# Opening of a two-block transformer layer: the first RMS norm moved behind the transposes and behind the products

## The chip, the cores and the metric

The kernel runs on 1 core of one Trainium2 chip. The core has TensorE (PE, with its weight loads PEld), VectorE (DVE), ScalarE (ACT), GpSimd (POOL) and SyncE (SP, which here only issues transfers), which run side by side and wait for each other by semaphores. The metric is the device time of one execution in microseconds (us); the kernel before takes 884.37 us as the median of 3 runs (884.16 to 885.26).

## The reference, cut to what matters

Two blocks follow each other. Only the head of the first is touched:

```python
def rmsnorm(x, g):
    y = x * lax.rsqrt(jnp.mean(x * x, axis=-1, keepdims=True) + EPS) * g
    return y

h = rmsnorm(x, g_mix_pre[l])            # x: 256 tokens x 1024, f32
proj = h @ w_in[l]                      # 1024 x 3080
# columns of proj: fq 512 | fk 512 | fv 512 | f_logit 8 | cq 512 | ck 512 | cv 512
y_fox = forgetting_attention(fq, fk, fv, f_logit + b_fgt)
y_chk = chunked_relpos_attention(cq, ck, cv, rel_bias)
```

After that come an output projection, attention over a memory, a feed-forward part, and a second block that is as long again. A token's factor 1/rms is one number per row of `h`, so it can be taken out of the product: `h @ w = (1/rms) * ((x * g) @ w)`.

## The kernel before

Everything is float32, and a product is made of three passes of a reduced format: each operand is split into a high part and the rest (hi, lo), and `mm3` issues hi x hi, hi x lo and lo x hi. ACT makes the hi part (a cast), DVE the lo part (a subtraction that reads the hi part). The weights come as units of 512 or 520 KB: SP loads a unit into one of four `raw` buffers, ACT makes `whi`, DVE makes `wlo`, and the buffer is free for the fourth unit after it. The 256 tokens are two halves, A and B, of 128 each; `ht` (tile `xb`) holds `h` transposed, eight tiles kt = 0 to 7 of 128 features, hi and lo.

The Python code is only the text from which a program is recorded: a small planner (`Kern`) keeps an estimate of each engine's clock and decides where the steps of side chains (norms, attention heads) are put between the products. The recorded order is fixed, each engine runs its own list strictly in order, and waits are semaphores. All instructions except products (L212, `mm`) and transposes (L225, `tr`) carry the line of one helper, L96, so groups are told apart by tile names.

The opening of `block1` in the kernel before, in order:

- SP loads the gain row `grow`, half B of `x`, and four units of `w_in`; ACT's queue loads half A of `x`.
- PE copies the gain to all partitions by a product with ones (`gb`). ACT squares and sums each half, POOL makes 1/rms (`rs`), DVE makes `xg` = x * rs * gain.
- PE transposes `xg`, 16 tiles of 128x128 into four PSUM banks (`tb`). ACT and DVE split each bank with one instruction each (128x512).
- Unit 0 is split by ACT and POOL, the other units by ACT and DVE.
- `gemm_n_skew` computes fv and f_logit (tile `gs`, two banks of 260 columns): four units for half A, then the same four for half B, 96 products in all.

Then the columns come in the order fq, fk (`gemm_t`, tile `gt`, results `qk`, each unit 24 products of 256 columns), cv (`gemm_n_inter`, tile `gn`), cq, ck (`gt`), and the two attentions run as side chains between the products. The forget gates need a running sum, `cps`, whose split form `ncum` enters the scores `s` of the first attention. ACT carries the results of fq, fk, cq and ck out of PSUM (`qk_evac`) and scales the queries by 0.125.

Of the kernel before, what the change touches and what calls it, by code (L numbers as in the profile page):

```python
# [21 lines left out]
EPS = 1e-6  # L22
N4, N2, NRAW = 33, 13, 4
# [15 lines left out]
def hs(half):  # L39
    return slice(half * P, half * P + P)  # L40
# [668 lines left out]
def block1(k, x, mem, w_in, b_fgt, rel, g_fox_out, g_chk_out, w_out, g_mix_pre, g_mix_post,  # L709
# [14 lines left out]
    gb = [k.bank(name="gb") for _ in range(2)]
    for j in range(2):
        k.mm(gb[j], k.ones[0:1, :], grow[:, j * 512:j * 512 + 512])
    xg, rs = [], []
    for half in range(2):
        xg.append(k.t4([P, D], name="xg"))
        ss, r = k.small(1, "ss"), k.small(1, "rs")  # L730
        nc.scalar.activation(xg[half], x0[half], AF.Square, scale=D ** -0.5, accum_out=ss)
        nc.gpsimd.tensor_tensor(r, ss, k.eps, op=OP.add)
        nc.gpsimd.tensor_tensor(r, r, k.mhalf[:, :1], op=OP.pow)
        rs.append(r)
    u = k.units
    k.split_hi(u[0])
    for kt in range(2):
        nc.gpsimd.tensor_tensor(u[0].lo[:, kt], u[0].raw[:, kt], u[0].hi[:, kt].bitcast(F32), op=OP.subtract)
    k.split_done()

    def norm_t(half, j):

        c = slice(j * 512, j * 512 + 512)
        nc.vector.scalar_tensor_tensor(xg[half][:, c], x0[half][:, c], rs[half], gb[j], op0=OP.mult, op1=OP.mult)
        ps = k.bank((P, 4, P), "tb")
        for i in range(4):
            k.tr(ps[:, i], xg[half][:, j * 512 + i * P:j * 512 + i * P + P])
        return ps

    def split_t(half, j, ps):  # L750
        split(k, ht.hi[j][:, :, hs(half)], ht.lo[j][:, :, hs(half)], ps)
        k.put()
    ps = [norm_t(half, j) for half in range(2) for j in range(2)]
    k.put(2)
    split_t(0, 0, ps[0])
    split_t(0, 1, ps[1])
    k.split_hi(u[1])
    k.split_lo(u[1])
    split_t(1, 0, ps[2])
    split_t(1, 1, ps[3])  # L760
    k.pump()
    setup_late(k)
# [10 lines left out]
    nc.gpsimd.memset(sp, 0.0)  # L773
# [3 lines left out]
    def fv_evac(half, j, ps):  # L777
        nc.scalar.copy(fv[:, half, 0:260], ps[0][:, :260])
        nc.scalar.copy(fv[:, half, 260:512], ps[1][:, :252])

        nc.vector.scalar_tensor_tensor(nx[:, half], ps[1][:, 252:260], -1.0, bf, op0=OP.mult, op1=OP.subtract)
        nc.vector.scalar_tensor_tensor(ax[:, half], nx[:, half], -1.0, nx[:, half], op0=OP.mult, op1=OP.min)


    gemm_n_skew(k, ht, 1, fv_evac, width=260, nb=2)
# [134 lines left out]
    gemm_n_inter(k, ht, lambda half, ps: nc.scalar.copy(cv[:, half], ps[0]))  # L920
# [986 lines left out]
```

## Time and profile before

| | us |
|---|---|
| median of 3 runs | 884.37 |
| the profiled execution | 884.47 |
| its span, first to last instruction | 882.7 |
| PE busy | 871.3 |
| DVE busy | 608.7 |
| ACT busy | 457.1 |
| POOL busy | 92.2 |

The profiled execution's own time is 1.8 us above its span; that rest lies around the instructions. Times in the rows count from the start of the span. The share of a busy PE says little by itself, because products are pipelined and their ends are modelled; what ends last is read from the chain of waits and from the idle time before single instructions.

### The profile page before, as it was taken

What the parts mean: (1) busy time and instruction counts of PE and PEld (TensorE: products, weight loads), DVE (VectorE), ACT (ScalarE), POOL (GpSimd) and SP (SyncE); (2) the same over time, 40 slices, a digit from 0 to 9 for tenths busy, and PEclk for the clock granted to TensorE, in tenths of its full rate; (3) what the DMA queues carried; (4) which work ended last, traced back from release to release, by engine and by line L of the source; (5) the groups of instructions that cost most, each with busy time, mean ns of one, the idle gap of its engine ahead of it and who ended that gap; (6) DMA issues with size and microseconds to landing.
All of it is one profiled execution on the core that took longest, in us unless ns stands there. A gap on an engine that the chain in (4) does not pass through costs nothing.

```text
span 882.7 us, 13878 instructions
## 1 busy us (share of the span) xinstructions
PE 871.3 (99%) x5320; PEld 754.4 (85%) x5320; DVE 608.7 (69%) x1076; ACT 457.1 (52%) x803; POOL 92.2 (10%) x150
## 2 busy tenths in 40 slices
PE   8999999999999999999999999999999999999998
PEld 6979998799788888888798899988987888888887
DVE  5675664765687667664769999979579786666661
ACT  6674654554476444442656665554564654444440
POOL 3101010200020000000100039800010000000000
PEclk9999999999999999999999999999999999999999
DMA  8992436473277766654551677395125586666521
GB/s 267 290 256 73 144 120 239 119 245 116 95 240 217 210 200 191 191 191 146 171 160 49 192 174 197 87 248 166 51 72 185 178 250 198 191 191 191 191 96 48
DMA packets 162612, 150.82 MB, mean 171 GB/s; under 512 B 20081, under 2 KB 127217, under 8 KB 162546
## 3 DMA queue, kind: packets, MB, share of 16 engines
q1 hardware_dynamic: 161970, 148.88, 56.7%
q10 hardware_dynamic: 576, 1.05, 0.4%
q8 instruction: 42, 0.69, 0.3%
q14 instruction: 24, 0.20, 0.1%
HBM read 148.08 MB, written 1.84 MB: 170 GB/s over the span
## 4 chain that ended last, share of the span: by engine, by line
PE 90%; DVE 4%; ACT 4%; issue 1%; DMA 0%; POOL 0%; DVEq 0%; ACTq 0%; POOLq 0%
PE gt L212 33%; PE acc L212 20%; PE gs L212 12%; PE gn L212 11%; PE tb L225 3%; PE mo L212 3%; DVE wlo L96 2%; PE o L212 1%; ACT whi L96 1%; ACT p L96 1%; ACT junk L96 1%; PE ops L212 1%; PE ms L212 1%; PE s L212 1%; DVE Z L96 1%
## 5 line engine op out<-in xcount | busy, mean ns | idle before, releaser
L96 DVE TENSOR_TENSOR wlo<-raw,whi 128x1024 fp32r<-128x1024 f32 (+1 forms) x263 | 316.4, 1225 | 107.6 <-ACT whi L96 98.6
L96 ACT CAST whi<-raw 128x1024 fp32r<-128x1024 f32 (+1 forms) x264 | 270.0, 1049 | 66.0 <-DMA raw<-in_w_in_dram 30.8
L212 PE MATMUL gt<-xb,whi 128*128 128x256 f32 (+1 forms) x1152 | 276.3, 322 | 0.0
L212 PE MATMUL gt<-xb,wlo 128*128 128x256 f32 x768 | 214.9, 280 | 0.0
L212 PEld LDWEIGHTS gt<-xb,whi 128*128 128x128 f32 x1152 | 190.0, 188 | 17.8 <-issue 1.0
L212 PEld LDWEIGHTS gt<-xb,wlo 128*128 128x128 f32 x768 | 144.6, 188 | 0.3
L212 PE MATMUL acc<-wlo,uh 128*128 128x512 f32 (+1 forms) x288 | 106.2, 369 | 0.0
L212 PE MATMUL acc<-whi,ul 128*128 128x512 f32 (+1 forms) x288 | 106.2, 369 | 0.0
L212 PE MATMUL acc<-whi,uh 128*128 128x512 f32 (+1 forms) x288 | 106.0, 368 | 0.0
L212 PE MATMUL gn<-whi,xb 128*128 128x512 f32 x256 | 90.8, 409 | 0.0
L212 PE MATMUL gs<-whi,xb 128*128 128x512 f32 (+1 forms) x288 | 85.8, 374 | 0.5 <-ACT xb L96 0.5
L212 PEld LDWEIGHTS acc<-whi,uh 128*128 128x128 f32 x288 | 54.2, 188 | 10.1
L212 PEld LDWEIGHTS acc<-whi,ul 128*128 128x128 f32 x288 | 54.1, 188 | 9.7
L212 PEld LDWEIGHTS acc<-wlo,uh 128*128 128x128 f32 x288 | 54.1, 188 | 9.6
L212 PEld LDWEIGHTS gs<-whi,xb 128*128 128x128 f32 x288 | 52.0, 188 | 10.9 <-ACT xb L96 1.0
L96 ACT COPY r<-gt 128x256 f32<-128x256 f32 x48 | 17.8, 371 | 83.5 <-PE gt L212 83.5
L212 PEld LDWEIGHTS gn<-whi,xb 128*128 128x128 f32 x256 | 48.2, 188 | 10.5 <-issue 0.7
L96 DVE TENSOR_TENSOR r<-gt,r 128x256 f32<-128x256 f32 x48 | 20.3, 423 | 49.3 <-ACT r L96 48.7
L212 PE MATMUL gs<-wlo,xb 128*128 128x512 f32 (+1 forms) x144 | 53.4, 371 | 0.8 <-DVE wlo L96 0.7
L96 POOL TENSOR_SCALAR ms<-ss 128x1 f32<-128x1 f32 x20 | 9.2, 458 | 420.4 <-ACT junk L96 420.3
L212 PE MATMUL gn<-wlo,xb 128*128 128x512 f32 x128 | 50.4, 394 | 0.0
L212 PEld LDWEIGHTS gs<-wlo,xb 128*128 128x128 f32 x144 | 27.1, 188 | 5.7 <-DVE wlo L96 1.4
(378 smaller groups left out, 1218.1 us busy)
## 6 DMA issues: line engine op xcount, KB each, us to landing
raw<-in_w_in_dram SPq DMA_DIRECT2D x84, 512.0 KB, 4.6
raw<-in_w_ff_dram SPq DMA_DIRECT2D x64, 512.0 KB, 4.6
raw<-in_w_mlp_up_dram SPq DMA_DIRECT2D x32, 512.0 KB, 5.4
raw<-in_w_mlp_down_dram SPq DMA_DIRECT2D x32, 512.0 KB, 3.4
raw<-in_w_out_dram SPq DMA_DIRECT2D x16, 512.0 KB, 3.9
raw<-in_w_mk_dram SPq DMA_DIRECT2D x8, 512.0 KB, 5.3
raw<-in_w_mv_dram SPq DMA_DIRECT2D x8, 512.0 KB, 4.0
raw<-in_w_mq_dram SPq DMA_DIRECT2D x8, 512.0 KB, 4.7
```

Source lines behind the costliest of these rows:

```text
L96: f(*args, **kw)
L212: self.nc.tensor.matmul(out, lhsT, rhs, start=start, stop=stop)
L225: self.nc.tensor.transpose(out, in_, self.ident[:n, :n])
```

## The change

The norm of the opening is taken apart.

- `x` is transposed as it comes (8 transposes of half A, later 8 of half B). The gain is loaded as 8 rows of 128 (`g8`), transposed once, and kept as `gT`, one number per partition and kt. It is applied when a transposed tile is split: ACT writes hi = tile * g, DVE writes lo = tile * g - hi. The split is now one 128x128 tile at a time.
- The weights of unit 0 are split in two halves, by ACT and DVE, between the tiles of half A; the lo part of unit 1 is made by POOL.
- Unit 0's load goes ahead of half B of `x` in SP's queue. The gain and memory loads for later (`bf`, `gkv`, `m0`) go ahead of unit 5 instead of behind unit 9.
- Products of half A with unit 0 come first, then the transposes of half B, then units 1 to 3.
- The squares and 1/rms come after the split of half B. 1/rms is kept per token on partitions (`rs`, `nrs`) and, by way of a small DRAM tile and a broadcast load on ACT's queue, as a row on every partition (`rrow`).
- 1/rms is applied as results leave PSUM: as the scale of ACT's copies for fv and cv, as a factor in DVE's `nx`, and for fq, fk, cq, ck by an instruction on DVE (128x512, `scalar_tensor_tensor` with `rrow`) that takes the place of ACT's copy.

```diff
+    g8 = k.t2([KT, P], name="g8")
+    nc.sync.dma_start(g8, bass.AP(tensor=g_mix_pre.tensor, offset=g_mix_pre.offset, ap=[[P, KT], [1, P]]))
     x0 = [k.t4([P, D], name="x0") for _ in range(2)]
-    grow = k.t4([1, D], name="grow")
-    nc.sync.dma_start(grow, g_mix_pre[None, :])
     nc.scalar.dma_start(x0[0], x[:P])
+    k._dma()
     nc.sync.dma_start(x0[1], x[P:])
...
-        nc.scalar.activation(xg[half], x0[half], AF.Square, scale=D ** -0.5, accum_out=ss)
...
-        nc.vector.scalar_tensor_tensor(xg[half][:, c], x0[half][:, c], rs[half], gb[j], op0=OP.mult, op1=OP.mult)
...
+    def split_x(half, ps, kts):
+        for kt in kts:
+            hi, lo = ht.x(kt, half)
+            g, src = gT[:, kt:kt + 1], ps[kt // 4][:, kt % 4]
+            nc.scalar.activation(hi, src, AF.Copy, scale=g)
+            nc.vector.scalar_tensor_tensor(lo, src, g, hi.bitcast(F32), op0=OP.mult, op1=OP.subtract)
...
+    ps = transpose_x(A)
+    split_x(A, ps, (0, 1))
     for kt in range(2):
+        nc.scalar.copy(u[0].hi[:, kt], u[0].raw[:, kt])
+        split_first(u[0], kt, nc.vector)
+        split_x(A, ps, (2 + kt,))
+    split_x(A, ps, range(4, 8))
...
+    nc.scalar.copy(u[1].hi, u[1].raw)
+    for kt in range(2):
+        split_first(u[1], kt, nc.gpsimd)
...
+    for i in range(4):
+        if i == 1:
+            psb = transpose_x(B)
+            split_x(B, psb, range(4))
+        parts.append(k.part())
+        k.held += 1
+        if i == 2:
+            split_x(B, psb, range(4, 8))
+            for half in range(2):
+                rstd(half)
+            nc.gpsimd.tensor_scalar(nrs, rs, -1.0, None, op0=OP.mult)
+        mm_n(k, ps, ht, A, parts[i], 2 * i, 260)
+    fv_evac(A, ps)
...
+    for half in range(2):
+        nc.scalar.dma_start(rscr[hs(half)][:, None], rs[:, half:half + 1])
...
+    nc.scalar.dma_start(rrow, bass.AP(tensor=rscr.tensor, offset=rscr[0:1].offset, ap=[[0, P], [1, S]]))
...
-            nc.scalar.activation(t[:, 2 * i:2 * i + 2], ps, AF.Copy, scale=scale)
+            nc.vector.scalar_tensor_tensor(t[:, 2 * i:2 * i + 2], ps, scale, mid(rrow, 2), op0=OP.mult, op1=OP.mult)
```

What ACT's list holds in the opening of the kernel before, from its first work on (`xb` is the transposed `h`, `tb` the PSUM bank of transposes; the brackets name what a row waits for, a transfer or an engine):

```order
L96 ACTIVATE xg,ss<-x_74 128x1024 [waits DMAHW1_49]
L96 ACTIVATE xg,ss<-x_75 128x1024 [waits DMAHW2_49]
L96 CAST whi<-raw 128x1040 [waits DMAHW3_49]
L96 CAST xb<-tb 128x4x128 [waits PE_49] x2
L96 CAST whi<-raw 128x1040 [waits DMAHW4_49]
L96 CAST xb<-tb 128x4x128 [waits PE_49] x2
L96 CAST whi<-raw 128x1040 [waits DMAHW5_49]
```

Two whole banks are cast by waiting for PE alone, and the third weight unit is cast after half B. The same place of ACT's list in the changed kernel:

```order
L96 ACTIVATE xb<-tb,gT 128x128 [waits PE_49]
L96 ACTIVATE xb<-tb,gT 128x128 [waits DVE_49]
L96 CAST whi<-raw 128x520 [waits DMAHW2_49]
L96 ACTIVATE xb<-tb,gT 128x128 [waits DVE_49]
L96 CAST whi<-raw 128x520
L96 ACTIVATE xb<-tb,gT 128x128 [waits DVE_49]
L96 ACTIVATE xb<-tb,gT 128x128 [waits PE_49]
L96 ACTIVATE xb<-tb,gT 128x128 [waits DVE_49] x3
L96 CAST whi<-raw 128x1040 [waits DMAHW4_49]
L96 ACTIVATE xb<-tb,gT 128x128 [waits PE_49]
L96 ACTIVATE xb<-tb,gT 128x128 [waits DVE_49] x3
L96 CAST whi<-raw 128x1040 [waits DMAHW5_49]
```

The first tile of a bank waits for PE, which signals once for four transposes; each further tile of the same bank waits for DVE, and the count it waits for is that of the lo part of the tile before. Unit 1 stands behind all eight tiles of half A, unit 2 behind four tiles of half B as well.

On DVE, shortly before the scores of the first attention, the difference of the two lists reads (`ncum` is the split running sum of the forget gates, `qk` here the first result of cq):

```order
+L96 TENSOR_TENSOR xlo<-tb,xhi 128x4x128
+L96 TENSOR_TENSOR wlo<-raw,whi 128x1024
 L96 TENSOR_TENSOR xlo<-tb,xhi 128x4x128 x3
+L96 TENSOR_TENSOR wlo<-raw,whi 128x1024 x2
+L96 SCALAR_TENSOR_TENSOR qk<-gt,rrow 128x512
+L96 TENSOR_TENSOR wlo<-raw,whi 128x1024
 L96 CAST ncum<-ch 128x128
 L96 TENSOR_TENSOR ncum<-cps,ch 8x128
```

The six `ncum` instructions now stand behind a `qk` that waits for the 48th product of cq, and behind one `wlo` more. On PE the scores moved too: they follow the 63rd product of cq, where in the kernel before they stood between the last products of cv. From the output projection on, PE's list is the same.

## Rows read from the trace of the kernel before

**Rows 1.** The page: busy time, share, instructions; granted clock in 40 slices, tenths.
```profile
PE 871.3 (99%) x5320; PEld 754.4 (85%) x5320; DVE 608.7 (69%) x1076; ACT 457.1 (52%) x803; POOL 92.2 (10%) x150
...
PEclk9999999999999999999999999999999999999999
```

**Rows 2.** Chain that ended last, first 60 us: start, length (us), what.
```profile
13.58 1.17 DVE wlo L96
...
14.79 8.78 PE gs L212 x71
23.57 22.58 PE gt L212 x192
```

**Rows 3.** Waits of PE to 120 us: total us, times, longest.
```profile
PE gs L212 <- DVE wlo L96: 0.7, 1, 0.7
PE o L212 <- DVE pt L96: 0.5, 1, 0.5
```

**Rows 4.** Timeline of PE: start, us, line, operation, count [idle before, releaser].
```profile
7.37 3.62 PE L225 MATMUL tb<-ident,xg 128*128 128x128 f32 x16 [0.41 <-DVE xg L96]
10.69 0.41 PE L212 MATMUL gs<-whi,xb 128*128 128x260 f32 x1
...
14.79 0.39 PE L212 MATMUL gs<-wlo,xb 128*128 128x260 f32 x1 [0.66 <-DVE wlo L96]
...
23.41 0.40 PE L212 MATMUL gt<-xb,whi 128*128 128x256 f32 x2
```

**Rows 5.** Groups by form, PE, 0 to 11 us: busy us, mean ns.
```profile
L225 PE MATMUL tb<-ident,xg 128*128 128x128 f32 x16 | 3.6, 421 | 0.4 <-DVE xg L96 0.4
```

**Rows 6.** Tile tb, whole span: duration ns min/median/max, first and last start.
```profile
L225 PE MATMUL tb<-ident,xg x96: 270/272/474, 7.4 to 710.1; 128*128 128x128 f32 x96
```

**Rows 7.** Timeline of ACT, opening.
```profile
4.40 1.06 ACT L96 ACTIVATE xg<-x 128x1024 f32<-128x1024 f32 x1 [1.92 <-DMA x<-in_x_dram]
...
5.67 1.06 ACT L96 ACTIVATE xg<-x 128x1024 f32<-128x1024 f32 x1
...
7.58 1.06 ACT L96 CAST whi<-raw 128x1040 fp32r<-128x1040 f32 x1 [0.76 <-DMA raw<-in_w_in_dram]
```

**Rows 8.** Groups by form, ACT, whole span.
```profile
L96 ACT COPY r<-gt 128x256 f32<-128x256 f32 x48 | 17.8, 371 | 83.5 <-PE gt L212 83.5
...
L96 ACT ACTIVATE cy<-gt,cw 128x256 f32<-128x256 f32 x24 | 10.1, 475 | 26.8 <-PE gt L212 26.7
...
L96 ACT COPY ikT<-tb 128x128 f32<-128x128 f32 x2 | 0.5, 262 | 0.0
```

**Rows 9.** Groups by form, DVE, whole span.
```profile
L96 DVE SCALAR_TENSOR_TENSOR r<-r 128x512 f32<-128x512 f32 x24 | 16.6, 692 | 0.8
...
L96 DVE SCALAR_TENSOR_TENSOR U<-gp,nci,QE 128x128 f32<-128x128 f32 x16 | 4.3, 344 | 0.0
...
L96 DVE TENSOR_TENSOR wlo<-raw,whi 128x1040 fp32r<-128x1040 f32 x3 | 3.8, 1299 | 0.3 <-ACT whi L96 0.3
```

**Rows 10.** Timeline of ACT, 292 to 304 us.
```profile
295.01 0.38 ACT L96 COPY r<-gt 128x256 f32<-128x256 f32 x1 [4.75 <-PE gt L212]
...
299.39 0.62 ACT L96 CAST uh<-r 128x512 fp32r<-128x512 f32 x1 [1.22 <-DVE r L96]
```

**Rows 11.** Timeline of DVE, 292 to 304 us.
```profile
295.42 0.42 DVE L96 TENSOR_TENSOR r<-gt,r 128x256 f32<-128x256 f32 x1 [3.89 <-ACT r L96]
...
298.66 0.69 DVE L96 SCALAR_TENSOR_TENSOR r<-r 128x512 f32<-128x512 f32 x1
```

**Rows 12.** Timeline of POOL, opening.
```profile
8.72 2.56 POOL L96 TENSOR_TENSOR wlo<-raw,whi 128x520 fp32r<-128x520 f32 x2 [0.99 <-ACT whi L96]
```

**Rows 13.** Timeline of SP's queue.
```profile
20.25 1.71 SPq L96 DMA_DIRECT2D bf<-in_b_fgt_dram  x1
```

**Rows 14.** Timeline of DVE before the first scores.
```profile
56.32 0.22 DVE L96 CAST ncum<-ch 128x128 fp32r<-128x128 f32 x1
...
57.68 0.28 DVE L96 TENSOR_TENSOR ncum<-cps,ch 8x128 fp32r<-8x128 f32 x1
```

More of the change, by code (lines that the diff above doesn't have):

```diff
@@ L722, in block1 @@
     ht = XT(k)
[L724 to L730, printed above, removed]
-        nc.scalar.activation(xg[half], x0[half], AF.Square, scale=D ** -0.5, accum_out=ss)
-        nc.gpsimd.tensor_tensor(r, ss, k.eps, op=OP.add)
-        nc.gpsimd.tensor_tensor(r, r, k.mhalf[:, :1], op=OP.pow)
-        rs.append(r)
@@ L735, in block1, with transpose_x @@
-    u = k.units
-    k.split_hi(u[0])
+    gps = k.bank(name="g8t")
+    k.tr(gps[:, :KT], g8, KT)
+    gT = k.keep([P, KT], "gT")
+    nc.vector.tensor_copy(gT, gps[:, :KT])
+    k.put()
+    u = k.units
+    def transpose_x(half):
+        ps = [k.bank((P, 4, P), "tb") for _ in range(2)]
+        for kt in range(KT):
+            k.tr(ps[kt // 4][:, kt % 4], x0[half][:, kt * P:kt * P + P])
+        return ps
+    def split_x(half, ps, kts):
[4 more added lines that the diff above has]
+            nc.vector.scalar_tensor_tensor(lo, src, g, hi.bitcast(F32), op0=OP.mult, op1=OP.subtract)
+            if kt % 4 == 3:
+                k.put()
@@ L739, in block1 @@
+    split_x(A, ps, range(4, 8))
     k.split_done()
-    def norm_t(half, j):
-        c = slice(j * 512, j * 512 + 512)
-        nc.vector.scalar_tensor_tensor(xg[half][:, c], x0[half][:, c], rs[half], gb[j], op0=OP.mult, op1=OP.mult)
[L745 to L762, printed above, removed]
     bf = k.keep([P, 8], "bf")
@@ L768, in block1, with rstd @@
         nc.sync.dma_start(m0[half], mem[half * P:half * P + P])
+    nc.scalar.copy(u[1].hi, u[1].raw)
+    for kt in range(2):
+        split_first(u[1], kt, nc.gpsimd)
+    k.split_done()
+    rs, nrs = k.keep([P, 2], "rs0"), k.keep([P, 2], "nrs0")
+    def rstd(half):
+        sq, ss = k.t4([P, D], name="sq"), k.small(1, "ss")
+        nc.scalar.activation(sq, x0[half], AF.Square, scale=D ** -0.5, accum_out=ss)
+        nc.gpsimd.tensor_tensor(ss, ss, k.eps, op=OP.add)
+        nc.gpsimd.tensor_tensor(rs[:, half:half + 1], ss, k.mhalf[:, :1], op=OP.pow)
@@ L785, in block1, with fv_evac @@
-    gemm_n_skew(k, ht, 1, fv_evac, width=260, nb=2)
+    def fv_evac(half, ps):
+        r = rs[:, half:half + 1]
+        nc.scalar.activation(fv[:, half, 0:260], ps[0][:, :260], AF.Copy, scale=r)
+        nc.scalar.activation(fv[:, half, 260:512], ps[1][:, :252], AF.Copy, scale=r)
+        nc.vector.scalar_tensor_tensor(nx[:, half], ps[1][:, 252:260], nrs[:, half:half + 1], bf, op0=OP.mult,
+                                       op1=OP.subtract)
+        nc.vector.scalar_tensor_tensor(ax[:, half], nx[:, half], -1.0, nx[:, half], op0=OP.mult, op1=OP.min)
+        k.put(2)
@@ new lines, in block1 @@
+    parts, ls, k.ls = [], k.ls, 1
+    ps = [k.bank(name="gs") for _ in range(2)]
+    for i in range(4):
[11 more added lines that the diff above has]
+    fv_evac(A, ps)
@@ new lines, in block1 @@
+    k.ls = ls
+    rrow = k.keep([P, S], "rrow")
+    rscr = k.dram.tile([S], F32, name="rscr")
+    for half in range(2):
+        nc.scalar.dma_start(rscr[hs(half)][:, None], rs[:, half:half + 1])
+    ps = [k.bank(name="gs") for _ in range(2)]
+    for i in range(4):
+        k.drop()
+        mm_n(k, ps, ht, B, parts[i], 2 * i, 260)
+    fv_evac(B, ps)
+    nc.scalar.dma_start(rrow, bass.AP(tensor=rscr.tensor, offset=rscr[0:1].offset, ap=[[0, P], [1, S]]))
+    k.tick()
+    setup_late(k)
+    nc.gpsimd.memset(sp, 0.0)
@@ L919, in block1 @@
     cv = k.t4([P, 2, 512], name="cv")
-    gemm_n_inter(k, ht, lambda half, ps: nc.scalar.copy(cv[:, half], ps[0]))
+    gemm_n_inter(k, ht, lambda half, ps: nc.scalar.activation(cv[:, half], ps[0], AF.Copy,
+                                                              scale=rs[:, half:half + 1]))
     cq, ev = qk_evac(0.125)
```

12 lines of the change are left out of this document (5 added, 7 removed).

## The prediction

> **What bounds the kernel now.** I read the busy times first: PE works in 871.3 of 882.7 us, so time is won or lost only where PE stands or where its list gets longer [rows 1]. The chain of waits then says where the opening hangs. A `wlo` on DVE ends at 14.75, the products of `gs` follow it to 23.5, and from 23.57 the products `gt` run through; up to 58 us PE carries the chain alone [rows 2]. Up to 120 us PE waits for other engines only in two places worth naming: 0.7 us for that `wlo`, and 0.5 us for a `pt` in the first attention [rows 3].
>
> PE's timeline gives the measure for the opening. The first `gs` product starts at 10.69, but it isn't the one to look at: at 14.79 a product waits for `wlo` of unit 2, and from there PE has 72 products of `gs` to do without another gap, ending at 23.41 where `gt` begins [rows 4]. 72 is the 96 products less the 24 of units 0 and 1 on half A. In the changed kernel the product with unit 2's `wlo` again has 71 others behind it in that stage. So the question is when **`wlo` of unit 2** ends: every us later than 14.75 is a us on PE's path. That PE starts earlier on unit 0 decides nothing, if it then waits.
>
> **The opening, step by step.** Half A of x has landed when ACT starts on it at 4.40 [rows 7]; its transfer is unchanged. PE then transposes x instead of waiting for the norm. The 16 transposes of the kernel before took 421 ns each, start to end, and 3.62 us in all, 0.21 us from one to the next [rows 4, 5]; so the fourth ends at 4.40 + 3 x 0.21 + 0.42 = 5.46. The gain's small load lies in SP's queue first and its copy waits for nobody late; I cost it at nothing, hidden by the wait for x.
>
> From here ACT and DVE alternate, since each further hi of a bank waits for the lo before it. Prices: an ACT copy of 128x128 out of PSUM takes 262 ns, and a scale that is a column per partition adds 475 - 371 = 104 ns at 256 columns, so hi = 0.37 [rows 8]; a `scalar_tensor_tensor` of 128x128 with a column per partition takes 0.34 = lo [rows 9]. A hand-over costs 0.03 (295.39 to 295.42) to 0.04 (299.35 to 299.39) [rows 10, 11]. One pair is 0.37 + 0.34 + 2 x 0.04 = **0.79 us**, where before one cast of 0.6 covered four tiles.
>
> What is removed (the products with ones, the early squares and powers, DVE's four `xg`) all lay ahead of 10.69; that it is gone is in these 5.46 us already.
>
> - hi0 starts at 5.50; two pairs end at 7.02. hi2 runs 7.07 to 7.44. Meanwhile ACT casts unit 0's halves (7.16 and 7.96) and DVE's lo parts of them, 0.7 each, stand in the list: lo2 ends at 8.15, lo3 at 9.01, behind them. Unit 0 must have landed by 6.5. It now takes the place of half B of x, which was in by 5.67, against 7.58 for unit 0 before [rows 7].
> - hi4 is in a new bank and waits for no lo; lo4 ends at 9.27. Three pairs more put the end of hi7 at 11.23.
> - Unit 1's cast (1.06 [rows 7]), issued 0.1 before hi7 ends, ends at 12.2.
> - Half B: hi0 starts at 12.12, three pairs, hi3 ends at 14.82.
> - Unit 2's cast follows to 15.80, its `wlo` (1.30) to **17.14** [rows 9].
>
> So `wlo` of unit 2 ends at 17.14 instead of 14.75: **+2.4 us**. Behind it nothing later binds in this stage: unit 3's `wlo` ends at 18.35 when PE needs it at 18.6; half B's last lo at 20.94, needed after 24; unit 4's `wlo` at 25.12, after two squares of 1.25 on ACT, needed at 25.8, when `gt` starts. That last cover is thin, 0.7 us. POOL's two halves of unit 1 (1.3 each) end near 14.8 and let PE finish unit 1 at 15.5, before 17.14 [rows 12]. The eight transposes of half B, now inside the stage, take 1.7 us from about 10.7 and lie in PE's wait for POOL. Lower bound: if the column costs nothing, each of nine chained hi is 0.1 shorter, +1.5. Upper: hand-overs of 0.07, +3.0.
>
> **The row of 1/rms.** Two writes to DRAM stand in ACT's list ahead of unit 5's cast, the broadcast load behind half B's evacuation. Issuing took 0.38 us on SP for most transfers, 1.71 for the small `bf` [rows 13]; I take 0.4 each, so unit 5's `wlo` ends near 27.4, needed at 28.6; at 1.7 each it would be late by 1.5. The row itself lands some 5 us after the evacuation, and the first `qk` is needed only in the attention, tens of us later. POOL's constants for the attentions now come behind 1/rms, near 24 us, and are needed there only tens of us later, too. SP's queue is no worse off: unit 5's load waits for POOL's part of unit 1, with ten us in hand.
>
> **From ACT to DVE.** Eight evacuations leave ACT and add 8 x 0.69 = 5.5 us to DVE [rows 9]. Up to the first scores DVE has slack on average, and PE has up to six units in hand, so most costs nothing. One place doesn't: `ncum` now stands behind the first `qk` of cq and one `wlo`. PE finishes the 48th product of cq, then has 15 more, 15 x 0.118 = 1.8 us [rows 2], before the scores, which need `ncum`. DVE needs 0.2 for the result to arrive, 0.69 for `qk`, 1.2 for the `wlo`, and 57.96 - 56.32 = 1.64 for `ncum` [rows 14], less overlaps 3.6 us. PE stands for **1.8 us** where it didn't stand before. Against that the scores of two pairs now stand together, with more products behind, and the 0.5 us wait for `pt` may go [rows 3]: net +1.3, between -0.5 (no stall, wait gone) and +1.8.
>
> **Sum.** 2.4 + 1.3 = +3.7. On the profiled execution of 884.47 (span 882.7 and 1.8 around it) that is 888.2; the median lies 0.1 below the profiled one, so 888.1.
>
> **The rule that speaks against the change.** Before, one instruction of each engine took a whole bank, so no row of before shows ACT and DVE wanting one bank for different tiles; the waits in the order are all I have. The Trainium skill, page "PSUM — Partial Sum Buffer", section "PSUM bank collisions raise a hardware error", states that two engines must not touch the same bank and quadrant at once, reads included, and that tools add a dependency for it. By that rule the alternation can't be short-cut and the sum is the one above; without it hi would run on alone, and the first rival's time would follow. That puts the first rival's chance low.
>
> **Rivals.**
>
> - *The alternation is cheap, not slower.* Place: the pairs of hi and lo. Some 7.5 pairs lie on the way to `wlo` of unit 2, so it breaks even at 0.79 - 2.4 / 7.5 = 0.47 us a pair. At 0.35, near what hi alone takes, PE's list itself becomes the bound and `gt` starts at 22.6, 0.8 earlier; with the `pt` wait gone too, 884.4 - 1.3 = 883.1. For it: PE's first product comes at 7.2 instead of 10.69. Against it: 0.37 and 0.34 are measured and the waits are in the list.
> - *Half of each cost.* The column costs ACT nothing (+1.5) and DVE reaches `ncum` in time (-0.5): 885.4. For it: my stall at `ncum` rests on the order alone.
> - *The clock.* The granted clock is full in every slice [rows 1], yet transposes took 421 ns in the opening and 272 in the median of the span, 0.21 us apart and not half of that [rows 4 to 6]; I read that as 1.2 GHz first and 2.4 GHz later. The 16 transposes ran nearly without a gap, and the products of `gs` after them are 0.12 apart [rows 2]. After the change PE has gaps at 6.3, 12 and 15.5. If it is still at 1.2 GHz when it resumes at 17.14, and for some 3.3 us, as long as those transposes lasted, half of that is lost: +1.6, 889.7. For it: the gaps. Against it: PE is dense from 7.9 to about 12. The Trainium skill, page "TensorE: Matmul & The Clock Gate", section "Part 1: The HAM clock gate", says the slow level is the default and activity releases it; the trace agrees with 421 against 272 ns.
> - *The DRAM writes are slow to issue* and unit 5 comes late: +1.5, 889.6.
>
> **How the numbers follow.** Forecast 0.48, clock 0.14, slow issue 0.06: slower, 0.68. Half costs 0.22 and part of the cheap alternation, 0.04: within 0.2%, 0.26. The rest of the cheap one, with a further wait of PE gone, 0.06: faster. 0.2% is 1.8 us, about what a measurement here can tell from no change. The range takes in half costs and, at the top, +3.0 and +1.8 with half the clock's price: 884.4 to 890.2.
>
> **What would show it.** Right: `wlo` of unit 2 ends near 17.1, `gt` starts near 25.8, hi and lo of one bank never overlap in time, and PE waits about 1.8 us for `ncum` at the first scores. Wrong: hi instructions 0.2 us apart, `gt` before 23.4, or no wait at the scores. Products of `gs` 0.22 apart after 17 us would speak for the clock; a wait of `gt` for unit 5 would speak for the DRAM writes.

## The result, and the profile after

The changed kernel takes **899.06 us** (median, 897.61 to 901.91) against 884.47 for the kernel before on the same chip: ratio 1.0167, interval 1.0156 to 1.0178. It is slower, as forecast, but by 14.6 us where 3.7 were forecast. The profiled execution spans 900.2 us against 882.7, 17.5 more; it is the longest of the five (901.91 us), so its pieces add up to some 3 us more than the median's.

The page of the changed kernel, busy time and granted clock, to be laid beside [rows 1]:

```profile
PE 876.9 (97%) x5317; PEld 759.7 (84%) x5317; DVE 613.0 (68%) x1094; ACT 455.4 (51%) x808; POOL 95.8 (11%) x151
...
PEclk9996999999999999999999999999999999999999
```

PE has three instructions fewer and is busy 5.6 us longer; the fourth slice (67 to 90 us) has a clock of 0.6. So the loss is early, partly time in which PE stands and partly time in which it works at half its clock. PE's timeline at the three points that can be laid beside the kernel before (columns as in [rows 4]):

```profile
16.11 0.63 PE L212 MATMUL gs<-whi,xb 128*128 128x260 f32 x2
17.27 0.45 PE L212 MATMUL gs<-wlo,xb 128*128 128x260 f32 x1 [0.52 <-DVE wlo L96]
17.56 0.40 PE L212 MATMUL gs<-whi,xb 128*128 128x260 f32 x2
...
25.93 0.40 PE L212 MATMUL gt<-xb,whi 128*128 128x256 f32 x2
...
79.08 0.66 PE L212 MATMUL s<-ncum,sel 128*128 128x384 f32 x1 [6.84 <-DVE ncum L96]
...
233.02 0.58 PE L212 MATMUL mo<-whi,xhi 128*128 128x512 f32 x1
```

and the last of them in the kernel before:

```profile
216.17 0.58 PE L212 MATMUL mo<-whi,xhi 128*128 128x512 f32 x1
```

Unit 2's `wlo` lets PE go at 17.27, and `gt` starts at 25.93 instead of 23.41: the opening costs **2.5 us**. The first `mo` product, whose place among the products is the same in both kernels, starts at 233.02 instead of 216.17. That is 16.8 later, and only 0.7 is added in the 660 us behind it. So some 14 us arise between 26 and 233, and the row at 79.08 shows the largest piece: PE stands **6.84 us** for `ncum`. The granted clock around it (windows: busy us and instructions of PE, PEld, DVE, ACT, POOL, then PEclk, DMA share, GB/s):

```profile
70.00:80.00 10.00, 3.16 (x24) 2.79 (x22) 5.62 (x10) 3.41 (x4) 0.31 (x1) 0.77 0.79 228
80.00:89.00 9.00, 9.00 (x42) 6.11 (x43) 2.30 (x8) 5.65 (x18) 0.00 (x0) 0.50 0.18 53
89.00:93.00 4.00, 4.00 (x37) 3.67 (x36) 2.64 (x5) 0.00 (x0) 0.00 (x0) 0.99 0.00 0
```

After the stall PE is busy without a gap from 80 to 89 at half its clock, 42 instructions in 9 us, where 37 take 4 us afterwards. About 10 us of work at half speed are 5 us lost.

What `ncum` waited for is told by the chain of waits of the changed kernel (start, length, what):

```profile
26.77 11.44 DMA raw<-in_w_in_dram
...
40.56 5.45 DMA raw<-in_w_in_dram
...
63.05 10.25 DMA raw<-in_w_in_dram
73.32 1.05 ACT whi L96
74.40 0.37 DVE wlo L96
```

Up to 58 us the chain of the kernel before is PE alone [rows 2]; here loads of weights stand in it. In windows from 18 to 38 us, DMA moves almost nothing for twelve of them (last column, GB/s):

```profile
18.00:22.00 4.00, 4.00 (x36) 4.00 (x35) 1.68 (x5) 2.50 (x6) 0.19 (x1) 1.00 1.05 288
22.00:26.00 4.00, 4.00 (x36) 4.00 (x35) 2.11 (x4) 3.92 (x7) 3.56 (x9) 1.00 0.22 47
26.00:30.00 4.00, 4.00 (x36) 4.00 (x36) 3.20 (x3) 1.38 (x2) 3.28 (x4) 1.00 0.62 26
30.00:34.00 4.00, 4.00 (x36) 4.00 (x36) 0.00 (x0) 0.00 (x0) 0.00 (x0) 1.00 0.74 39
34.00:38.00 4.00, 3.85 (x31) 3.50 (x30) 0.46 (x1) 1.05 (x1) 0.00 (x0) 1.00 0.99 269
```

In the same windows of the kernel before it moves 294, 257, 364, 320 and 234 GB/s; the two that matter most read:

```profile
26.00:30.00 4.00, 4.00 (x36) 4.00 (x35) 3.67 (x6) 0.99 (x3) 0.00 (x0) 1.00 1.00 364
30.00:34.00 4.00, 4.00 (x36) 4.00 (x35) 0.50 (x1) 1.05 (x1) 0.00 (x0) 1.00 1.13 320
```

The first four of the twelve, 22 to 26 us, are a hole that the first version below, which has no writes to DRAM, shows as well (27 GB/s); the eight behind them are not. The two columns to compare are the last two: from 26 to 34 us the DMA engines are *busy* for two thirds of the time and move a tenth of what they moved before. The view of the DMA issues (tile, queue, count, KB each, us from issue to landing) says of 26 to 34 us, and of 22.5 to 24 us:

```profile
raw<-in_w_in_dram SPq DMA_DIRECT2D x3, 512.0 KB, 11.4
```

```profile
rscr<-rs ACTq DMA_DIRECT2D x2, 0.5 KB, 8.4
```

and in the kernel before, of 26 to 34 us:

```profile
raw<-in_w_in_dram SPq DMA_DIRECT2D x3, 512.0 KB, 6.9
```

The two writes of 1/rms to DRAM, 512 bytes each in 128 words of 4 bytes, take 8.4 us, and the weight loads issued behind them 11.4 instead of 6.9. In the packets of the trace, single packets of 512 bytes, whose median is 27 ns and of which none took over 0.7 us from 10 to 26 us, took up to 4.8 us between 26 and 34 us. ACT waits 9 us for the load of unit 8 (timeline):

```profile
36.46 1.05 ACT L96 CAST whi<-raw 128x1024 fp32r<-128x1024 f32 x1 [9.08 <-DMA raw<-in_w_in_dram]
```

So by 58 us the changed kernel has loaded 13.42 MB and the kernel before 15.79: 2.4 MB behind, 8 us at 290 GB/s, with loads that already run at about that rate.

### The profile page after: what moved, and what is told of

The parts are those of the page before. It is cut to its first block, busy times and chain, and to the rows that moved or that the text cites. A ratio compares the mean times of both kernels' runs of the same rounds, so it can differ in the third digit from the quotient of the medians.

```text
span 900.2 us, 13898 instructions
## 1 busy us (share of the span) xinstructions
PE 876.9 (97%) x5317; PEld 759.7 (84%) x5317; DVE 613.0 (68%) x1094; ACT 455.4 (51%) x808; POOL 95.8 (11%) x151
## 4 chain that ended last, share of the span: by engine, by line
PE 81%; DVE 7%; ACT 5%; DMA 4%; issue 2%; ACTq 0%; DVEq 0%
PE gt L212 27%; PE acc L212 20%; PE gs L212 10%; PE gn L212 10%; DVE wlo L96 3%; DMA raw<-in_w_in_dram 3%; PE tb L225 3%; PE mo L212 3%; ACT whi L96 2%; PE s L212 1%; ACT p L96 1%; PE o L212 1%; ACT junk L96 1%; PE ops L212 1%; DMA raw<-in_w_mo_dram 1%
## 5 line engine op out<-in xcount | busy, mean ns | idle before, releaser
L212 PE MATMUL gs<-whi,xb 128*128 128x512 f32 (+1 forms) x288 | 88.4, 382 | 1.4 <-ACT whi L96 0.9
L212 PEld LDWEIGHTS gs<-whi,xb 128*128 128x128 f32 x288 | 54.0, 196 | 12.3 <-ACT whi L96 1.5
L212 PEld LDWEIGHTS acc<-whi,uh 128*128 128x128 f32 x288 | 54.2, 188 | 10.2
L96 POOL TENSOR_SCALAR ms<-ss 128x1 f32<-128x1 f32 x20 | 11.3, 565 | 421.2 <-ACT junk L96 421.1
```

Of the source, the lines that this page charges most:

```text
L96: f(*args, **kw)
L212: self.nc.tensor.matmul(out, lhsT, rhs, start=start, stop=stop)
```

## Experiments

Two theories. **A**: the 256 small writes jam the weight loads, and the late loads do the rest. **B**: the scaled evacuations on DVE, and with them DVE's order of work, are the price, and the jam is covered. All times below are medians; the kernel before ran beside each group and took 884.3 to 885.2 us.

### The row of 1/rms without DRAM

```diff
-    rscr = k.dram.tile([S], F32, name="rscr")
+    rd = k.t4([P, 2, P], name="rd")
     for half in range(2):
-        nc.scalar.dma_start(rscr[hs(half)][:, None], rs[:, half:half + 1])
+        nc.scalar.activation(rd[:, half], k.ident, AF.Copy, scale=rs[:, half:half + 1])
...
-    nc.scalar.dma_start(rrow, bass.AP(tensor=rscr.tensor, offset=rscr[0:1].offset, ap=[[0, P], [1, S]]))
+    rps = k.bank(name="rps")
+    k.mm(rps[:, :S], k.ones, flat(rd))
+    nc.scalar.copy(rrow, rps[:, :S])
...
```

> The changed kernel, with the row of 1/rms made without DRAM: two 128x128 diagonal blocks on ACT, one fp32 matmul of 256 columns against the ones, one copy of 128x256 on ACT. All else stays, the scaled evacuations of q and k on DVE among it. Theory A (the 256 writes of 4 bytes jam the loads: the packets of units 8 to 10 took up to 4.8 us each between 25.5 and 34.5 us, about 40 GB/s where the loads before them had 300): the loads of units 8 and 9 land within 6 us of their issue instead of 11.7, ACT's 9.1 us of idle time before unit 8 shrinks to under 4, the 6.8 us before the first scores shrink to under 2.5, and the time is 886 to 890. Theory B (DVE is the bound, by the scaled evacuations and its order of work between 44 and 68 us, and the jam is covered by what lies between): PE still stands 5 us or more before the first scores and the time is 896 or more.

Measured: **894.85** (ratio 1.0118, interval 1.0103 to 1.0133), 4.2 less than the changed kernel, between the two theories. The jam is gone: the loads issued from 20 to 36 us land in 4.8 us, and by 58 us 15.17 MB are in. But PE still stands 3.29 us before the first scores. The rows of ACT and DVE ahead of that show why, and it is not load:

```profile
64.33 0.69 ACT L96 ACTIVATE cv<-gn,rs 128x512 f32<-128x512 f32 x1 [0.33 <-PE gn L212]
64.91 1.04 ACT L96 CAST whi<-raw 128x1024 fp32r<-128x1024 f32 x1
```

```profile
65.98 1.23 DVE L96 TENSOR_TENSOR wlo<-raw,whi 128x1024 fp32r<-128x1024 f32 x1 [2.25 <-ACT whi L96]
67.12 0.22 DVE L96 CAST ncum<-ch 128x128 fp32r<-128x128 f32 x1
```

DVE stands idle for 2.25 us with `ncum` ready to run (its input `ch` was copied at 63.62), because a `wlo` is ahead of it whose `whi` is behind a `cv` evacuation on ACT. So there is a third thing, the **place of `ncum`** in DVE's order. And not all else stayed: with the edit the planner also gave another order. Here one `wlo` stands ahead of `ncum` and 12 products of cq ahead of the scores; in the changed kernel these are three `wlo`, a `qk` and 63 products, and `ch` stands behind one `whi` more on ACT. So the 4.2 us are the price of the words and of this change of order together. This run's opening was also worse than the changed kernel's: `gt` starts at 27.82, 1.9 later, with PE at half its clock.

### The small writes alone, in the kernel before

```diff
+    rscr = k.dram.tile([S], F32, name="rscr")
+    rrow = k.keep([P, 8], "rrow")
+    def words():
+        for half in range(2):
+            nc.scalar.dma_start(rscr[hs(half)][:, None], rs[half])
-    gemm_n_skew(k, ht, 1, fv_evac, width=260, nb=2)
+    gemm_n_skew(k, ht, 1, fv_evac, width=260, nb=2, before_b=words)
+    nc.scalar.dma_start(rrow, bass.AP(tensor=rscr.tensor, offset=0, ap=[[0, P], [1, 8]]))
```

> The kernel before, with nothing added but the two writes of 128 words of 4 bytes each to DRAM, issued on ACT behind the first half's `fv` evacuation at about 21 us; nobody reads them. Theory A: the raw loads issued behind them land 4 us or more later than the 5.5 us of before, their packets take over 1 us at places, and the time rises by 3 to 9 us (887.5 to 893.5), since the loads run at 290 GB/s from 2 to 64 us and have nothing to make up the loss with. Theory B: the loads stay near 5.5 us or the loss is covered, and the time is within 0.5 us of the kernel before.

Measured: **888.55** (1.0055, 1.0037 to 1.0072): 256 words of 4 bytes, 1 KB in all, cost **4.2 us** in a kernel that doesn't use them, and PE, ACT and POOL have the same order as before. (The last line of the edit, which the expectation left out, loads 4 KB of them back. It is issued at 28.19, and in the trace its packets move from 32.3 us on; by 30 us 7.27 MB are in where the kernel before has 8.35, so the harm to the loads is done ahead of it.) The windows behind the writes, the first two in GB/s 275 and 145:

```profile
20.00:24.00 4.00, 4.00 (x35) 4.00 (x35) 1.22 (x1) 2.18 (x5) 0.00 (x0) 1.00 1.45 275
24.00:28.00 4.00, 4.00 (x36) 4.00 (x35) 0.00 (x0) 0.66 (x2) 0.00 (x0) 1.00 0.90 145
```

Of the load packets, some took up to 3.0 us. PE then stands 1.7 us for `ncum` where it stood for nothing before, and from 62 to 66 its granted clock is 0.57. Theory A, as far as it goes. That the harm is of the same size as what the row by PE gained is chance, since the row by PE had another order too.

### Two packets instead of 256

```diff
-    rscr = k.dram.tile([S], F32, name="rscr")
-    for half in range(2):
-        nc.scalar.dma_start(rscr[hs(half)][:, None], rs[:, half:half + 1])
+    rscr = k.dram.tile([2, P], F32, name="rscr")
+    rps = k.bank(name="rps")
+    k.tr(rps[:2, :P], rs, P)
+    rt = k.keep([2, P], "rt")
+    nc.scalar.copy(rt, rps[:2, :P])
...
+    nc.scalar.dma_start(rscr, rt)
...
```

> The changed kernel with the same trip through DRAM, but the two columns of 1/rms transposed by PE first, so that it writes 2 rows of 512 bytes instead of 256 words of 4 bytes; the read back is the same. Theory A in its narrow form (the many small writes are the harm): as the row by PE, 886 to 890, and no gap in the loads. If the harm lies in the trip through DRAM itself (the wait for the write, the 128 KB read back at 38 us), it stays at 896 or more.

Measured: **895.22** (1.0117, 1.0100 to 1.0134). By the time alone neither side is told apart, for my edit brought a wait of its own: PE stands 3.3 us at 20 us for POOL's `rs`, since its transpose is in order ahead of `gs`. The loads answer the question: those issued from 22 to 36 us land in 5.0 us, and DMA moves 237 and 289 GB/s from 26 to 34 us, where the changed kernel moves 26 and 39. The trip through DRAM with the same read back does not jam; the words do.

### No row at all

```diff
-    rrow = k.keep([P, S], "rrow")
-    rscr = k.dram.tile([S], F32, name="rscr")
...
-            nc.vector.scalar_tensor_tensor(t[:, 2 * i:2 * i + 2], ps, scale, mid(rrow, 2), op0=OP.mult, op1=OP.mult)
+            nc.scalar.activation(t[:, 2 * i:2 * i + 2], ps, AF.Copy, scale=scale)
```

> The changed kernel without the row: no DRAM trip, and q and k evacuated by ACT with the constant scale as in the kernel before, so that their 1/rms is left out of the computation. What is left is the opening in its new form and the scaled `fv` and `cv`. Theory A: the 2.5 us of the opening (`gt` starts at 25.93 instead of 23.41) and little else, 886 to 888; the difference to the row by PE is then the price of the scaled evacuations on DVE, 0 to 2 us. Theory B: the same 886 to 888 here, but 8 us or more below the row by PE.

Measured: **889.48** (1.0056, 1.0041 to 1.0071), 1.5 above the upper end expected; the profiled execution, the shortest of the four with 888.41 (span 886.1), had `gt` at 25.86 (+2.5) and a wait of 1.0 for `ncum`, and PE at full clock from there to the end. Of the other three, two have a lower mean granted clock on record (0.996 at 890.08, 0.998 at 889.32, against 1.0); what the third had in addition, 889.64 at full clock, isn't in a trace. To the row by PE it is 5.4 less, which looked like the price of DVE's evacuations until the next two runs.

### `ncum` behind its input

```diff
         nc.scalar.copy(ch, cps[:, :S])
-        yield ch
```

The line gives the chain back to the planner, which goes on with it when its own clock says that `ch` is there. Without it, `ncum` is written right behind. First with the words left in:

> The changed kernel with the 256 words left in, and `ncum` written right behind the copy of `ch` instead of when the planner's clock comes to it. On DVE two `wlo` and one `qk` no longer stand ahead of `ncum`, and some 36 `gt` of `cq` move behind the first scores on PE. Theory A as far as it got (the words cost 4 us by themselves, the rest is the place of `ncum` behind work whose loads are late): one `wlo` whose load is late may still stand ahead, the wait of 6.8 us before the first scores becomes 1 to 4 us, PE's time at the lower clock shrinks with it, and the time is 889 to 895. If the late loads alone are the cause, PE runs dry a little later on the next `wlo`, and the time stays at 897 or more.

Measured: **901.94** (1.0193, 1.0176 to 1.0210), no better than the changed kernel, and a miss. PE's wait grew to 8.8 us. ACT's timeline shows that I had moved the wrong half of the chain:

```profile
70.78 1.04 ACT L96 CAST whi<-raw 128x1024 fp32r<-128x1024 f32 x1 [3.50 <-DMA raw<-in_w_in_dram]
71.73 0.37 ACT L96 CAST ch<-cps 128x256 fp32r<-128x256 f32 x1
```

`ch` itself stands on ACT behind a `whi` whose load is late. And as the scores moved ahead of 54 `gt` (I had written 36), PE ran out of work earlier, at 66.06 instead of 72.24. Then without the words:

> The row by PE and `ncum` early together: one `wlo`, whose `whi` stands on ACT behind a `cv` evacuation, goes behind `ncum`. The row by PE alone took 894.9, with 3.3 us before the first scores, 6.8 us of PE at half its clock behind that, and in its profiled run 6.8 us at half clock in the opening. Expected: the wait before the first scores under 1 us, no fall of the clock there, and 887 to 890 (the opening's 2.5 us, up to 2 us more where the clock falls in the opening, and 1 us of scaled evacuations). If the scaled evacuations on DVE are the price by themselves, and not the place of `ncum`, it stays at 893 or more.

Measured: **890.20** (1.0055, 1.0040 to 1.0070), 4.7 less than the row by PE, 0.2 above the upper end expected; the wait is 1.27 where under 1 was expected, with no fall of the clock there. The scaled evacuations are still all on DVE, and only 0.7 us is left between this run and the one without a row. So of theory B the load of the evacuations falls, and DVE's order stays. Between this run and the one with the words left in lie 901.94 - 890.20 = 11.7 us, but again not words alone: there `ch` stands behind a `whi` and `ncum` behind a `wlo` that don't stand ahead of them here. At last with `ch` moved too, words left in:

```diff
-        yield cps
         ch = k.t2([P, S], F32R, name="ch")
         nc.scalar.copy(ch, cps[:, :S])
-        yield ch
```

> The changed kernel with the 256 words left in, and both `ch` on ACT and `ncum` on DVE written right behind `cps`, so that neither engine has a late `whi` or `wlo` ahead of them. With `ncum` alone moved, the time stayed at 901.9: `ch` itself stood on ACT behind a `whi` that waited 3.5 us for its load, and PE stood 8.8 us. Theory A now says that the late loads do the harm only through what stands behind them in ACT's and DVE's queues: the wait before the first scores falls under 2 us, and the time is 891 to 896 (the row by PE with `ncum` early took 890.2, the words cost 4.2 us in the kernel before). If PE runs out of split units as well, whatever the order, it waits on `whi` or `wlo` a little later, and the time stays at 898 or more.

Measured: **895.99** (1.0121, 1.0107 to 1.0135), the upper end. No late load stands ahead of `ch` (63.83) any more, yet PE waits 3.7 us where under 2 were expected: `ncum` starts at 65.97 behind a backlog of DVE, which works without a gap from 59.3 to 67.7 on what the late loads had pushed together. So late loads reach PE in two ways, by standing ahead in a queue and by bunching the work behind them; the order decides how much of it is paid. The order is nearly that of the run before it, with the row by PE and `ncum` early, which makes this the nearest price of the words in the changed kernel: 895.99 - 890.20 = **5.8 us** (rather too little, since the opening of that run has a stretch at half the clock, shown under the two banks).

### One bank or two

```diff
-            k.tr(ps[kt // 4][:, kt % 4], x0[half][:, kt * P:kt * P + P])
+            k.tr(ps[kt % 2][:, kt // 2], x0[half][:, kt * P:kt * P + P])
...
-            g, src = gT[:, kt:kt + 1], ps[kt // 4][:, kt % 4]
+            g, src = gT[:, kt:kt + 1], ps[kt % 2][:, kt // 2]
...
```

This is an edit of the row by PE with `ncum` early (890.20).

> As the one before, and consecutive 128-column blocks of the transposed x go to two PSUM banks in turn, so that ACT's `hi` of a block and DVE's `lo` of the one before it read different banks; the order of instructions on PE, ACT and DVE is the same. If ACT and DVE take turns because of the bank, a pair falls from 0.79 to about 0.45 us, `wlo` of unit 2 ends near 15 instead of 17.1, `gt` starts 1.5 to 2.5 us earlier than 25.9, and the time is 1.5 to 3 us under the one before. If they take turns for another reason (ACT waits for DVE's semaphore whatever the bank), the pairs stay at 0.79 and the two times agree within 0.7.

Measured: **886.75** (1.0017, 1.0007 to 1.0026), 3.4 less than the one it edits, where 1.5 to 3 were expected. The instructions of PE, ACT and DVE stand in the same order. ACT in the changed kernel (one bank):

```profile
9.48 0.37 ACT L96 ACTIVATE xb<-tb,gT 128x128 fp32r<-128x128 f32 x1 [0.50 <-DVE xb L96]
10.27 0.37 ACT L96 ACTIVATE xb<-tb,gT 128x128 fp32r<-128x128 f32 x1 [0.42 <-DVE xb L96]
11.05 0.37 ACT L96 ACTIVATE xb<-tb,gT 128x128 fp32r<-128x128 f32 x1 [0.42 <-DVE xb L96]
```

and with two banks, ACT and DVE:

```profile
12.32 0.62 ACT L96 ACTIVATE xb<-tb,gT 128x128 fp32r<-128x128 f32 x2 [1.01 <-PE tb L225]
13.11 0.62 ACT L96 ACTIVATE xb<-tb,gT 128x128 fp32r<-128x128 f32 x2 [0.16 <-DVE xb L96]
```

```profile
12.72 0.61 DVE L96 SCALAR_TENSOR_TENSOR xb<-tb,gT,xb 128x128 fp32r<-128x128 f32 x2 [1.98 <-ACT xb L96]
13.51 0.61 DVE L96 SCALAR_TENSOR_TENSOR xb<-tb,gT,xb 128x128 fp32r<-128x128 f32 x2 [0.18 <-ACT xb L96]
```

One `hi` every 0.79 us becomes two (12.32 to 13.11), and ACT and DVE overlap. The bank was the reason. But the gain through it is smaller than 3.4: `gt` starts at 24.86, 1.0 earlier than the changed kernel's 25.93, since ACT now waits for PE's transposes (the 1.01 above) and unit 2's `wlo` ends only some 1.3 earlier. The other 1.9 of the 2.9 between the two profiled openings (27.80 and 24.86) is the clock. Windows of the version with one bank, whose `gt` starts at 27.80, show it:

```profile
11.00:14.00 3.00, 1.47 (x10) 1.03 (x9) 1.05 (x3) 2.16 (x5) 1.65 (x2) 1.00 0.92 302
14.00:21.00 7.00, 6.36 (x29) 5.76 (x28) 4.41 (x8) 4.25 (x9) 0.89 (x1) 0.52 1.00 317
21.00:25.00 4.00, 4.00 (x35) 4.00 (x34) 1.31 (x2) 4.00 (x10) 2.91 (x7) 0.98 0.37 105
```

PE was granted the full clock at 11 us, stood for half of the three us up to 14, and then had half the clock for 7 us. So not all of the 3.4 is the bank's: the one of its four executions whose mean granted clock was full took 888.61, 1.9 above the version with two banks.

### How the words must lie to do harm

```diff
-    rscr = k.dram.tile([S], F32, name="rscr")
+    rscr = k.dram.tile([S, P], F32, name="rscr")
...
-            nc.scalar.dma_start(rscr[hs(half)][:, None], rs[half])
+            nc.scalar.dma_start(rscr[hs(half), 0:1], rs[half])
```

The kernel before with the same 256 words, each 512 bytes from the next, and then (`[S, 16]`) 64 bytes. The diff is against the version with the words in a row; the load back is left out as well:

> The kernel before with the same 256 writes of 4 bytes at the same place, but each word 512 bytes from the next in DRAM; nothing is read back. The 256 words in one row cost 4.2 us (888.55 against 884.34) and made packets of the loads take up to 3.0 us. If the harm is that neighbouring words share a piece of DRAM, it is gone here: within 0.7 us of the kernel before, no load packet over 1.4 us. If 256 small writes are the harm wherever they go, 887 to 890 again.

> The kernel before with the 256 words written 64 bytes apart. In one row (4 bytes apart) they cost 4.2 us and packets of the loads took up to 3.0 us; 512 bytes apart they cost 0.3. If the harm comes from words that share 64 bytes, it is gone here as well (within 0.7 us of the kernel before); if it takes a larger piece of DRAM to be shared, 886 to 889 with load packets of over 1.4 us.

Measured: **885.28** (1.0004, 0.9994 to 1.0013) and **885.96** (1.0007, 0.9998 to 1.0016; by the medians 0.8 above the kernel before, where up to 0.7 was expected). The window that moved 145 GB/s with the words in a row, at 512 and at 64 bytes:

```profile
24.00:28.00 4.00, 4.00 (x37) 4.00 (x36) 1.79 (x4) 2.64 (x4) 0.00 (x0) 1.00 0.74 268
```

```profile
24.00:28.00 4.00, 4.00 (x36) 4.00 (x35) 1.23 (x3) 2.65 (x4) 0.00 (x0) 1.00 1.01 318
```

By 30 us 8.25 and 8.29 MB are in, of 8.35 in the kernel before. The writes land in 4.5 and 4.8 us, and no load packet takes over 1.4 us. As many packets of the same size into the same DRAM do no harm that the intervals show when they lie 64 bytes apart: it is neighbouring words that do. Distances between 4 and 64 bytes weren't tried. The Trainium skill, page "DMA: Bandwidth & Descriptors", section "Specifications", puts the least transfer for full rate at 512 bytes, with reading, changing and writing back below it. These runs agree that small writes can be costly (4.2 us), but where I would read the page as all three kernels paying, only the one whose words lie 4 bytes apart pays measurably. That such words queue up on one piece of DRAM is my reading; the runs show the distance and the price, not the mechanism.

### What is left of the opening

```diff
-        for kt in range(KT):
+        for kt in (0, 2, 4, 6, 1, 3, 5, 7):
             k.tr(ps[kt % 2][:, kt // 2], x0[half][:, kt * P:kt * P + P])
```

> As the two banks (886.75), with the transposes of a half written bank by bank (blocks 0, 2, 4, 6, then 1, 3, 5, 7), so that the first `hi` waits for four transposes instead of seven or eight. The first `hi` starts at about 5.6 us instead of 6.17, the first `gs` near 6.9 instead of 7.36, and the time is 0.3 to 0.7 us under the two banks, if the opening of PE still sets the end; the same as the two banks, if the wait only goes to unit 1's `wlo` (POOL) or unit 2's.

Measured: **886.65** (1.0015, 1.0006 to 1.0024). The first `hi` starts at 5.62 as expected, the first `gs` at 7.41 as before, and nothing is won: what was late next is unit 0's `whi`.

```diff
+    warm = k.bank(name="warm")
+    for i in range(3):
+        k.mm(warm[:, :P], k.ones, k.ones, True, True)
     k.tr(gps[:, :KT], g8, KT)
+    for i in range(4):
+        k.mm(warm[:, :P], k.ones, k.ones, True, True)
```

> As the one before, and PE multiplies the ones by themselves (7 fp32 products of 128 columns, into a bank that nobody reads) between 1 and 4.4 us, where it else stands still for the loads of g and x. In the changed kernel the matmuls up to 17.3 us ran at the lower clock (0.64 us for a pair that takes 0.40 later), in the two banks up to 12.1, in the kernel before, with four fp32 products from 3.2 us, up to 10.8. If PE's own work before the first product decides when the clock rises, it is at full clock from 8 us or before and `gt` starts 1 us or more earlier than in the one before, 884 to 886; if the clock rises when it will, the two agree within 0.5.

Measured: **887.23** (1.0021, 1.0012 to 1.0030), no better than the one without, a miss. The clock did rise earlier: the first `gs` product takes 0.38 us, and 0.59 in the one without. But the products themselves were in the way: they run until 5.5 us, so the transposes of x start at 5.29 instead of 4.47 and the first `gs` at 8.06 instead of 7.41. And the clock fell again (windows):

```profile
7.00:10.00 3.00, 1.68 (x10) 1.31 (x10) 2.46 (x7) 2.38 (x7) 0.00 (x0) 1.00 1.05 408
10.00:17.00 7.00, 6.22 (x30) 5.83 (x29) 4.88 (x11) 5.57 (x12) 2.55 (x2) 0.52 0.86 289
17.00:21.00 4.00, 4.00 (x35) 4.00 (x34) 1.16 (x5) 3.77 (x8) 1.57 (x5) 0.99 1.14 324
```

PE at full clock ran ahead of ACT's splits, stood in 1.3 of the 3 us up to 10, and got half the clock until 17. Last, two changes of order that were to remove the waits still left, PE's 1.27 for `ncum` and 0.9 for unit 2's `wlo`:

```diff
                                     op=OP.subtract)
         k.put()
+        yield 1.5
```

> The even-and-odd version (886.65), with the first scores put on PE 12 triples... of `gt` products later in the order (36 more `gt`, about 4.3 us of work), so that `ncum` has time to come. If PE's 1.27 us before the first scores is a matter of place alone, it goes, and the time is 885.0 to 886.0; if the chain of `cps`, `ch` and `ncum` is only late next for something behind it (the second scores, `pt`), it stays at 886.3 or more.

```diff
             psb = transpose_x(B)
-            split_x(B, psb, range(4))
         parts.append(k.part())
         k.held += 1
+        if i == 1:
+            split_x(B, psb, range(4))
```

> As the one before, and on ACT and DVE the split of unit 2 goes ahead of the first four blocks of the second half's x, which nobody needs before the second half's products. `wlo` of unit 2 ends some 2 us earlier than 15.9, PE's 0.89 us of waiting there goes, `gt` starts near 24.0 instead of 24.8, and the time is 0.5 to 0.9 us under the one before, about level with the kernel before (884.3 to 885.3). If the loads set the pace there (unit 2's load lands only near 13 us), ACT waits for it and nothing is won, and the time is the same as the one before within 0.4.

Measured: **887.01** (1.0043, 1.0026 to 1.0059) and **891.21** (1.0058, 1.0041 to 1.0075). In the first, 18 more `gt` stand ahead of the scores (I had written 36), the wait for `ncum` is gone, and PE waits a little later:

```profile
PE o L212 <- DVE pt L96: 1.8, 1, 1.8
```

In the second the wait for unit 2's `wlo` falls from 0.4 to 0.2, that for POOL's parts of unit 1 rises from 1.0 to 2.0, and `gt` starts at 24.56 instead of 24.32. Their executions spread from 886.7 to 892.8 and from 887.4 to 892.2, and the traces are of the shortest or near it. What the long ones had is on record with each time: a mean granted clock of 0.994 to 0.996 in all that took over 890 us, 0.999 or 1.0 in all under 888. A mean of 0.994 over 890 us is up to 5.3 us lost, most of the spread; where in the kernel the clock fell isn't in a trace. Among those under 888 the second order is no better than the first (887.42 and 887.83 against 886.66 to 887.29). No version beat the kernel before.

## Why the prediction was right and wrong

- **The opening, +2.4: right**, by its own steps. Pairs of hi and lo 0.79 us (9.48 to 10.27), unit 2's `wlo` ends at 17.21 and PE goes on at 17.27 (17.14 forecast), `gt` at 25.93 (25.8). That ACT and DVE take turns because of the bank was argued before and is shown by the two banks. The Trainium skill, page "PSUM — Partial Sum Buffer", section "PSUM bank collisions raise a hardware error", has two engines kept from touching one bank at once; the trace agrees, with 0.79 us per block in one bank and 0.79 for two blocks in two.
- **The row of 1/rms: the step that failed.** I priced what the writes cost ACT to issue (0.4 each, from [rows 13]; issuing took 0.33 and 0.78) and when the row lands, and let the rival on unit 5 hang on the issue. What they do to the transfers behind them I didn't ask. Unit 5 wasn't late; the loads issued behind the writes were. From 26 to 34 us they moved 26 and 39 GB/s where the kernel before moves 364 and 320. Price: 4.2 us in the kernel before, in one and the same order; 5.8 in the changed kernel, in nearly the same order. The 4.2 from the changed kernel to the row by PE and the 11.7 further on hold a change of order as well.
- **"SP's queue is no worse off", "PE has up to six units in hand": wrong.** The loads are 2.4 MB behind by 58 us. The units in hand lasted until 38 us, where PE stood for unit 8:

```profile
38.82 0.38 PE L212 MATMUL gt<-xb,wlo 128*128 128x256 f32 x1 [0.75 <-DVE wlo L96]
```

  Nothing refilled them, for from 38 to 72 us DMA moved 264 GB/s, no more than the kernel before does (275 from 23 to 58). PE ran from 39 to 57 us without a wait, and paid at 72.
- **The wait for `ncum`: the place was right, the size wrong**, 6.84 us against 1.8. I summed DVE's own work ahead of it (`qk`, `wlo`, and `ncum` as in [rows 14]) as if its inputs were there. DVE's rows in the changed kernel show what the sum left out:

```profile
72.77 1.23 DVE L96 TENSOR_TENSOR wlo<-raw,whi 128x1024 fp32r<-128x1024 f32 x1 [5.08 <-ACT whi L96]
74.40 1.23 DVE L96 TENSOR_TENSOR wlo<-raw,whi 128x1024 fp32r<-128x1024 f32 x1 [0.41 <-ACT whi L96]
75.54 0.69 DVE L96 SCALAR_TENSOR_TENSOR qk<-gt,rrow 128x512 f32<-128x512 f32 x1
76.14 1.22 DVE L96 TENSOR_TENSOR wlo<-raw,whi 128x1024 fp32r<-128x1024 f32 x1
77.28 0.22 DVE L96 CAST ncum<-ch 128x128 fp32r<-128x128 f32 x1
```

  5.08 us of idle time for a split whose load landed late, then two more splits. No run took the words out with this order kept, so how much of the 6.84 the late loads cost alone stays open. Without the words and behind one `wlo`, without the `qk`, PE still stood 3.29; with `ncum` ahead of that `wlo` too, 1.27. So that one `wlo` ahead of `ncum` is worth 4.7 us (894.85 to 890.20), wait and clock together.
- **The clock: a rival with the right price in another place.** I gave +1.6 for a clock that stays low in the opening, 0.14. In the changed kernel's trace it rose at 17.4, in time; in the row by PE it cost 1.9 there. What I hadn't priced is that a stall of PE can bring the lower clock behind it: 5 us after the 6.84.
- **The sum.** From kernel to kernel: words, with the planner's new order, 899.06 - 894.85 = 4.2; place of `ncum` 894.85 - 890.20 = 4.7; one bank, with the clock in the opening, 890.20 - 886.75 = 3.4; what is left to the kernel before on the same chip, 886.75 - 885.03 = 1.7. Together 14.0; the kernel before took 0.56 more beside the last of them than beside the first (885.03 and 884.47), which makes the 14.6. The steps lead along one path; taken in another order they could be other numbers. (The top of the forecast's range, 3.0, 1.8 and half of 1.6 above 884.4, comes to 890.0 and not 890.2.)

## What to carry to other kernels

Price a transfer not by its issue and landing alone but by what is in flight beside it: look up the rate of the loads in that stage first, and where they run without a pause, time that a new transfer takes from them can come back later as a wait. Before moving an instruction behind others in an engine's queue, follow each of those back to its load, for it waits for the latest of them, and add what the clock takes after a stall. A row from a column of 128 numbers can be made by PE (a diagonal times ones) for under 2 us of ACT and PE; it should not go to DRAM word by word.

## What the runs showed that I had not expected

- 256 writes of 4 bytes to neighbouring DRAM words took the weight loads down to 26 and 39 GB/s for 8 us in the changed kernel (234 and 285 with the row by PE), with single packets of 512 bytes taking up to 4.8 us instead of 27 ns. In the kernel before the same words cost 4.2 us, and 64 bytes apart 0.8, within the interval of no change.
- PE's clock fell behind single stalls, but also behind a stretch with several gaps: a wait of 1.7 us was followed by about 3.4 us at half clock, one of 6.8 us by about 13.7 (the stall's last part among them), and 1.5 busy us in 3 by 7. It doesn't go by the length of the stall alone: 3.3 us brought 6.8 in the row by PE and 3.4 with two packets, 8.8 us brought 10.2 with `ncum` early, and waits of 1.27 and 1.8 us in two other runs brought none. Raising the clock early with idle products won nothing: they held up the transposes by 0.8 us, and PE then ran ahead of its inputs and stood.
